# Down projection of a streaming encoder layer: block sums of its weight by accumulating DMAs one product ahead, first product a11 b11

## Chip, core and metric

One of the eight cores of one Trainium2 chip runs the whole kernel. The time is what the device takes for one execution, in microseconds (us). The kernel before was run three times: 1790.78 us in the median, 1787.89 to 1794.69 us. A further execution was profiled. TensorE (PE) multiplies, VectorE (DVE), ScalarE (ACT) and GpSimd (POOL) work on tiles, and SyncE (SP) issues most of the DMAs.

## What is computed

One inference layer over 1024 prompt tokens and 32 sample tokens, T = 1056 together, width 1024, in float32. The change lies in the last matmul of the feed-forward block (FFN):

```
h = h + a @ w_o
f = rmsnorm(h)
gc = causal_dwconv3(f @ w_g)
y = (gelu(gc) * (f @ w_u)) @ w_d
h = h + y
h = h + (p @ w_pe) * sigmoid(rmsnorm(h) @ w_pg)
```

w_d has 2816 rows and 1024 columns. Everything before and after this matmul computes the same in both kernels.

## The kernel before

The activations lie transposed: features on the 128 partitions, tokens along a row. A float32 operand is split into two parts, hi (ACT, `split_x`, line 255) and lo = x - hi (DVE, line 256), and a product of two operands is three matmuls, hi hi, hi lo and lo hi (`mm3`, lines 248 to 250).

The FFN loop makes the rows of the hidden layer, 22 tiles of 128 features (`ly`), two per block. The matmul with w_d is a Strassen-Winograd product of 2 by 2 blocks: even and odd row tiles of w_d against its even and odd column tiles, and even and odd feature tiles against the two halves of the tokens (HT = 528 each). It takes seven products instead of eight. Their right-hand operands (b11, b21, b22 and the sums t1, t2, t3, t4) are made by DVE at the end of each FFN block (lines 1307 to 1310) and stored by SP to the scratch tensor `d_q`. Their left-hand operands are blocks of w_d and sums of blocks.

The stage runs over `PRODUCTS`, in each over four units u (two column tiles of w_d, so two tiles `hT[2u]`, `hT[2u+1]` of h), in each over two halves of 264 tokens, and in each over 11 feature pairs k, three matmuls each. So a unit is 66 matmuls and a product 264. One half of a unit fills one PSUM tile `gt` (three of them); then it is added into h or into `rr[u]`, which holds the product a11 b11 and what is added to it later.

- **Rows** of the next product, 11 of 264 KB, are loaded by `stage` into tiles M (`mtile`, three) and T (`stg`, four) and split by `split_row`. DVE's part of a split is ordered behind the last addition of a unit (`behind`): rows 0 to 3 behind unit 1, 4 to 7 behind unit 2, 8 to 10 behind unit 3.
- **Weights** of a unit, 704 KB, come by `raw_w` into two `wraw` tiles or one `wr` tile. Products t1 and t3 start a sum tile `wsum[u]` by one DMA and add a second block with POOL (`add_w`, line 1397); t2 and b22 add one more block each. `product_w` does this at the beginning of the unit that uses it, then splits the sum into six hi and six lo tiles, enough for two units.
- **h** was stored to `d_h` before the FFN. `hT`, the tile T, `r2` (which holds `rr[2]` and `rr[3]`) and the pool of `wsum` lie in memory that the tiles of the FFN held (`lps.close()`), so nothing is put there before the last `d_q` store has landed. `rr[0]` and `rr[1]` lie elsewhere.

A scheduler orders each engine's instructions by a simulated time line. Each engine, and SP as issuer of DMAs, then works in its order.

Of the kernel before, what the change touches and what calls it, by code (L numbers as in the profile page):

```python
# [9 lines left out]
F32 = mybir.dt.float32  # L10
F32R = mybir.dt.float32r
I32 = mybir.dt.int32
AF = mybir.ActivationFunctionType
ALU = mybir.AluOpType
AX = mybir.AxisListType

SEQ, DEC, D, PAST, FF, PED = 1024, 32, 1024, 2048, 2816, 256
T = SEQ + DEC
# [5 lines left out]
NB = NF // 2  # L24
HT = T // 2
# [57 lines left out]
def layer_kernel(ctx: ExitStack, tc: tile.TileContext, I, O):  # L83
# [26 lines left out]
    def load(out, in_):  # L110
        nc.sync.dma_start(out=out, in_=in_)
# [22 lines left out]
    def copy(out, in_):  # L134
        return S.activation(out, in_, AF.Copy)  # L135

    def after(ins, other):

        tc.add_manual_dep(ins.ins, other.ins.name,
                          mybir.DependencyInfo(mybir.DependencyClass.NoSync, mybir.DependencyReason.DATA),  # L140
                          reason="order")
        return ins
# [109 lines left out]
    def split_x(hi, lo, src, scale=None):  # L252

        if scale is None:
            S.activation(hi, src, AF.Copy)
            return V.tensor_tensor(out=lo, in0=src, in1=hi.bitcast(F32), op=ALU.subtract)  # L256
        else:
            S.activation(hi, src, AF.Copy, scale=scale)
            return V.scalar_tensor_tensor(out=lo, in0=src, scalar=scale, in1=hi.bitcast(F32),  # L259
                                   op0=ALU.mult, op1=ALU.subtract)  # L260

    def fm(get, j, xs, c0, n):

# [1012 lines left out]
    for b in range(NF // 2):  # L1276
        wg = strassen_w(I["w_g"][0], b * 256)
        gg = [ytile(1060) for _ in range(2)]
        for j in range(2):
            ft = 2 * b + j  # L1280
            V.memset(gg[j][:, 0:2], 0.0)
            V.tensor_copy(gg[j][:, 1026:1028], convw[:, 66 + ft:110:NF])
        strassen(wg, ops, put_rows([g[:, 2:1060] for g in gg], 2))
        ys = []
        for j in range(2):
            ft, g = 2 * b + j, gg[j]
            V.tensor_copy(cout[:, 0:2, ft], g[:, 1024:1026])
            V.tensor_copy(cout[:, 2:4, ft], g[:, 1058:1060])
            y = ytile(1060)[:, 0:1058]
            V.tensor_scalar(out=y, in0=g[:, 0:1058], scalar1=convw[:, ft:ft + 1], scalar2=convb[:, ft:ft + 1],  # L1290
                            op0=ALU.mult, op1=ALU.add)
            V.scalar_tensor_tensor(out=y, in0=g[:, 1:1059], scalar=convw[:, NF + ft:NF + ft + 1], in1=y,
                                   op0=ALU.mult, op1=ALU.add)
            V.scalar_tensor_tensor(out=y, in0=g[:, 2:1060], scalar=convw[:, 2 * NF + ft:2 * NF + ft + 1], in1=y,
                                   op0=ALU.mult, op1=ALU.add)
            S.activation(y, y, AF.Gelu_apprx_tanh)
            ys.append(y)
        wu = strassen_w(I["w_u"][0], b * 256)
        ss = [ytile() for _ in range(2)]
        strassen(wu, ops, put_rows(ss, 0))  # L1300
        for j, a, e, o in ((1, 0, HT, 0), (1, HT, SEQ, 0), (1, SEQ, T, 2), (0, 0, SEQ, 0), (0, SEQ, T, 2)):
            (V if b == NB - 1 else G).tensor_tensor(out=ss[j][:, a:e], in0=ss[j][:, a:e], in1=ys[j][:, a + o:e + o],
                                                    op=ALU.mult)

        (b11_, b12_), (b21_, b22_), (t3_, t1_) = ((x[:, 0:HT], x[:, HT:T]) for x in (ss[0], ss[1], ys[0]))
        t4_ = ys[1][:, 0:HT]
        V.tensor_tensor(out=t3_, in0=b22_, in1=b12_, op=ALU.subtract)
        V.tensor_tensor(out=t1_, in0=b11_, in1=b12_, op=ALU.subtract)
        V.tensor_tensor(out=b12_, in0=t3_, in1=b11_, op=ALU.add)
        V.tensor_tensor(out=t4_, in0=b12_, in1=b21_, op=ALU.subtract)  # L1310
        for n, x in ((0, ss[0]), (2, ss[1]), (4, ys[0])):
            load(q_rows(n, 2, b), x[:, 0:T].rearrange("p (n c) -> p n c", n=2))
        load(q_rows(6, 1, b), t4_.unsqueeze(1))

    ps = mt()
# [5 lines left out]

    PRODUCTS = ("b21", "b11", "t1", "t2", "b22", "t3", "t4")
    wsum = [None] * 4
    wv = I["w_d"][0].rearrange("(b j p) c -> j p b c", j=2, p=128)
    f2 = [None] * KD
# [39 lines left out]
    def split_row(n, b, raw, behind=None):  # L1367
        if n % 2 and b < 6:
            t = dn.tile([128, 2, HT], F32R, name="oq", tag="Q", bufs=6)
        else:  # L1370
            t = ap_.tile([128, 2, HT], F32R, name="oq", tag="A", bufs=16)
        ins = split_x(t[:, 0, :], t[:, 1, :], raw, -1.0 if PRODUCTS[n] == "t2" else None)
        if behind is not None:
            after(ins, behind)
        xo[n, b] = t

    nraw = [1]
# [14 lines left out]
        load(t.rearrange("p (k c) -> p k c", c=128), src)  # L1392
        return [t[:, 0:512], t[:, 512:1024], t[:, 1024:1408]]

    def add_w(dst, src):
        for x, y in zip(dst, src):
            G.tensor_tensor(out=x, in0=x, in1=y, op=ALU.add)
        return dst

    def product_w(n, u):  # L1400
        nm = PRODUCTS[n]
        if nm == "b21":
            w = raw_w(0, 1, u)
        elif nm == "b11":
            w = raw_w(0, 0, u)
        elif nm == "t4":
            w = raw_w(1, 1, u)
        elif nm == "t1":
            t = sb.tile([128, NB * 128], F32, name="wsum", tag="B", bufs=4)
            w = wsum[u] = add_w(raw_w(1, 0, u, own=t), raw_w(1, 1, u, wide=u % 2))  # L1410
        elif nm == "t2":
            w = add_w(wsum[u], raw_w(0, 0, u))
        elif nm == "b22":
            w = add_w(wsum[u], raw_w(0, 1, u))
        else:
            t = sb.tile([128, NB * 128], F32, name="wsum", tag="B", bufs=4)
            w = add_w(raw_w(1, 0, u, own=t), raw_w(0, 0, u, wide=u % 2))
        parts = []
        for x in w:
            c = x.shape[1]  # L1420
            hi = wp.tile([128, 512], F32R, name="whi", tag="hi", bufs=6)
            lo = wp.tile([128, 512], F32R, name="wlo", tag="lo", bufs=6)
            split_x(hi[:, :c], lo[:, :c], x)
            parts.append((hi, lo))
        return [tuple(y[:, k % 4 * 128:k % 4 * 128 + 128] for y in parts[k // 4]) for k in range(NB)]

    def acc_into(dst, src, op=ALU.add):
        return V.tensor_tensor(out=dst, in0=dst, in1=src, op=op)  # L1428

    for b in range(NB - 1):  # L1430
        stage(0, b)
    xo["raw", 0, NB - 1] = ss[1][:, 0:HT]
    for b in range(NB):
        split_row(0, b, xo.pop(("raw", 0, b)))

# [7 lines left out]

    for n, nm in enumerate(PRODUCTS):
        if n == 6:
            sbs.close()
            lp, ybufs = pool("last"), 5
        first = n == 0
        for u in range(4):
            ws = product_w(n, u)  # L1450
            he, ho = hT[2 * u], hT[2 * u + 1]
            if n < 2:
                m = 2 * u + n
                load(hT[m], d_h[m * 128:(m + 1) * 128, :])
            done = None
            for c0 in (0, SC):
                ps = gt(SC)
                mm3(ps, ws, [(xo[n, k][:, 0, c0:c0 + SC], xo[n, k][:, 1, c0:c0 + SC]) for k in range(NB)])
                a, b_ = slice(c0, c0 + SC), slice(HT + c0, HT + c0 + SC)
                if nm == "b21":  # L1460
                    done = acc_into(he[:, a], ps)
                elif nm == "b11":
                    copy(rr[u][:, a], ps)
                    done = acc_into(he[:, a], ps)
                elif nm == "t1":
                    acc_into(he[:, b_], ps)
                    done = acc_into(ho[:, b_], ps, ALU.subtract)
                elif nm in ("t2", "t3"):
                    done = acc_into(rr[u][:, a], ps)
                elif nm == "b22":  # L1470
                    done = acc_into(he[:, b_], ps)
                else:
                    acc_into(ho[:, a], ps, ALU.subtract)
            if nm == "t2":
                acc_into(he[:, HT:T], rr[u])
            elif nm == "t3":
                acc_into(ho[:, HT:T], rr[u], ALU.subtract)
                acc_into(ho[:, 0:HT], rr[u], ALU.subtract)
            if n < 6:

                for b in range(4 * u, min(4 * u + 4, NB)):
                    stage(n + 1, b)
                for b in range(4 * u - 4, min(4 * u, NB)):
                    if b >= 0:
                        split_row(n + 1, b, xo.pop(("raw", n + 1, b)), done)
            else:
                for m in ((0, 2), (4, 6), (1, 3), (5, 7))[u] if u < 3 else ():
                    fin(m)
# [64 lines left out]
```

## Time and profile before

| | |
|---|---|
| median of three runs | 1790.78 us |
| profiled execution, its own time | 1788.01 us |
| its span, first to last instruction | 1786.2 us |
| outside the span | 1.8 us |
| PE busy | 1734.9 us, 97% of the span |
| DVE busy | 1142.0 us, 64% |
| ACT busy | 764.5 us, 43% |
| POOL busy | 397.2 us, 22% |
| mean granted clock of TensorE | 0.991 of full speed |

Busy shares are means over stages. A matmul's own time overlaps the next one's, so idle time of PE and the granted clock tell more than its busy share. Times in the rows below count from the start of the span.

### The profile page before, as it was taken

Reading aid. Unit: us, or ns where it says so; the run is one execution under the profiler, and the core shown is the slowest. Engines: PE = TensorE matmul, PEld = TensorE weight load, DVE = VectorE, ACT = ScalarE, POOL = GpSimd, SP = SyncE. Lnnn points to the kernel's source line nnn. Section 1 sums busy time; section 2 is a strip of 40 time slices with the busy share of each in tenths; the row PEclk is TensorE's granted clock in tenths of the full one; section 3 lists DMA queues with packets and bytes.
Section 4 is the critical chain, followed back from the end, with each engine's and each line's share of the span. In section 5 each row is a group of like instructions: output and inputs, shape, how many; then the busy total and the mean of one; then the engine's idle time right before and its main releaser. Section 6 shows DMA issues by size and latency. Waiting matters only on the chain. (4 is left out here: it accounts for less than half of the span.)

```text
span 1786.2 us, 32756 instructions
## 1 busy us (share of the span) xinstructions
PE 1734.9 (97%) x12890; PEld 1704.0 (95%) x12890; DVE 1142.0 (64%) x2428; ACT 764.5 (43%) x1726; POOL 397.2 (22%) x410
## 2 busy tenths in 40 slices
PE   7999999999999999999999999999999889989998
PEld 6998999999999999999999999999999888989998
DVE  7766766666664564565468876666666647757643
ACT  6536564656324434322346444343433433334332
POOL 5110001000121021000002434444334006331111
PEclk9999999999999999999999999999999989999999
DMA  8311222212222214544453332223332596662431
GB/s 287 101 54 41 72 72 76 82 66 78 85 65 68 80 52 168 177 144 148 153 168 109 103 102 90 90 91 109 111 117 79 184 324 198 186 193 76 135 121 49
DMA packets 191822, 210.17 MB, mean 118 GB/s; under 512 B 11229, under 2 KB 156981, under 8 KB 191669
## 3 DMA queue, kind: packets, MB, share of 16 engines
q1 hardware_dynamic: 174936, 177.52, 31.7%
q0 software_dynamic: 8896, 26.06, 4.2%
q10 hardware_dynamic: 7837, 4.51, 0.9%
q8 instruction: 101, 1.65, 0.4%
q14 instruction: 52, 0.43, 0.1%
HBM read 151.99 MB, written 56.06 MB: 116 GB/s over the span
## 5 line engine op out<-in xcount | busy, mean ns | idle before, releaser
L248 PE MATMUL gt<-apair,whi 128*128 128x352 f32 x672 | 220.0, 328 | 0.1
L249 PE MATMUL gt<-apair,whi 128*128 128x352 f32 x672 | 219.3, 327 | 0.0
L250 PE MATMUL gt<-apair,wlo 128*128 128x352 f32 x672 | 218.7, 326 | 0.0
L1183 DVE TENSOR_TENSOR wlo<-wraw,whi 128x512 fp32r<-128x512 f32 x154 | 142.0, 930 | 91.8 <-ACT whi L1182 91.7
L248 PE MATMUL gt<-oq,whi 128*128 128x264 f32 x616 | 177.4, 291 | 16.9 <-DVE hT L1428 11.2
L249 PE MATMUL gt<-oq,whi 128*128 128x264 f32 x616 | 179.1, 292 | 11.6 <-DVE oq L256 10.8
L250 PE MATMUL gt<-oq,wlo 128*128 128x264 f32 x616 | 177.6, 290 | 0.0
L1182 ACT ACTIVATE whi<-wraw 128x512 fp32r<-128x512 f32 x154 | 96.3, 632 | 158.7 <-PE st L1224 66.5
L1223 PE MATMUL gt<-opt,whi 128*128 128x264 f32 x528 | 149.7, 284 | 0.7 <-ACT whi L1182 0.4
L1224 PE MATMUL gt<-opt,whi 128*128 128x264 f32 x528 | 149.9, 284 | 0.0
L1225 PE MATMUL gt<-opt,wlo 128*128 128x264 f32 x528 | 149.7, 284 | 0.0
L248 PE MATMUL gt<-whi,apair 128*128 128x256 f32 x512 | 147.1, 289 | 0.6 <-ACT whi L221 0.6
L250 PE MATMUL gt<-whi,apair 128*128 128x256 f32 x512 | 146.9, 287 | 0.9 <-POOL apair L384 0.6
L249 PE MATMUL gt<-wlo,apair 128*128 128x256 f32 x512 | 146.9, 287 | 0.0
L248 PEld LDWEIGHTS gt<-oq,whi 128*128 128x128 f32 x616 | 118.8, 194 | 17.9 <-DVE hT L1428 11.9
L249 PEld LDWEIGHTS gt<-oq,whi 128*128 128x128 f32 x616 | 119.2, 194 | 13.9 <-DVE oq L256 12.8
L250 PEld LDWEIGHTS gt<-apair,wlo 128*128 128x128 f32 x672 | 126.6, 188 | 1.9 <-issue 0.2
L249 PEld LDWEIGHTS gt<-apair,whi 128*128 128x128 f32 x672 | 126.6, 188 | 1.4
L248 PEld LDWEIGHTS gt<-apair,whi 128*128 128x128 f32 x672 | 126.2, 188 | 1.7 <-DVE etile L782 0.3
L250 PEld LDWEIGHTS gt<-oq,wlo 128*128 128x128 f32 x616 | 119.3, 194 | 0.2 <-DVE wlo L256 0.2
L221 ACT ACTIVATE whi<-wraw 128x512 fp32r<-128x512 f32 x152 | 91.8, 629 | 63.0 <-PE gt L249 58.5
L222 DVE TENSOR_TENSOR wlo<-wraw,whi 128x512 fp32r<-128x512 f32 x152 | 103.7, 702 | 14.8 <-ACT whi L221 11.8
(455 smaller groups left out, 5209.6 us busy)
## 6 DMA issues: line engine op xcount, KB each, us to landing
d_q<-ly SPq DMA_DIRECT2D x33, 528.0 KB, 3.7
wraw<-in_w_in SPq DMA_DIRECT2D x28, 512.0 KB, 3.9
wraw<-in_w_g SPq DMA_DIRECT2D x22, 512.0 KB, 3.9
wraw<-in_w_u SPq DMA_DIRECT2D x22, 512.0 KB, 4.3
mtile<-d_q SPq DMA_DIRECT2D x36, 264.0 KB, 3.3
d_gt<-etile POOLq DMA_DIRECT2D x48, 176.0 KB, 2.1
ly<-d_gt SPq DMA_DIRECT2D x16, 528.0 KB, 3.6
wr<-in_w_d SPq DMA_DIRECT2D x12, 704.0 KB, 6.9
```

What stands on the lines that cost most here:

```text
L221: S.activation(hi, r, AF.Copy)
L222: V.tensor_tensor(out=lo, in0=r, in1=hi.bitcast(F32), op=ALU.subtract)
L248: PE.matmul(ps, wh, xh, start=first and i == 0, stop=False)
L249: PE.matmul(ps, wh, xl, start=False, stop=False)
L250: PE.matmul(ps, wl, xh, start=False, stop=last and i == n - 1)
L1182: S.activation(h3, src, AF.Copy)
L1183: V.tensor_tensor(out=l3, in0=src, in1=h3.bitcast(F32), op=ALU.subtract)
L1223: PE.matmul(ps, wh[:, ws], xh, start=start and k == 0, stop=False, skip_group_check=True)
L1224: PE.matmul(ps, wh[:, ws], xl, start=False, stop=False, skip_group_check=True)
L1225: PE.matmul(ps, wl[:, ws], xh, start=False, stop=k == n - 1, skip_group_check=True)
```

## The change

- The first product is b11 instead of b21. It is only copied into `rr[u]` by ACT; before, b11 came second, was copied and also added to h. Now b21 comes second, is added to h, and at the end of each unit `rr[u]` is added to h in one piece. So no `hT` is needed in the first product.
- The last row of the first product is taken from SBUF: `ss[0]` instead of `ss[1]`, and the products of the hidden layer are made for `ss[0]` first.
- POOL adds no weight blocks. `w_sums` loads the first block into `wsum[u]` by SP and adds the other by a DMA on POOL's queue that accumulates into the tile. It is called one product before the sum is used, behind the split of the same unit.
- `split_x` returns both instructions, so that a row of the second product is ordered on ACT behind ACT's copy of the first.

```diff
-        for j, a, e, o in ((1, 0, HT, 0), (1, HT, SEQ, 0), (1, SEQ, T, 2), (0, 0, SEQ, 0), (0, SEQ, T, 2)):
+        for j, a, e, o in ((0, 0, HT, 0), (0, HT, SEQ, 0), (0, SEQ, T, 2), (1, 0, SEQ, 0), (1, SEQ, T, 2)):
...
-    PRODUCTS = ("b21", "b11", "t1", "t2", "b22", "t3", "t4")
+    PRODUCTS = ("b11", "b21", "t1", "t2", "b22", "t3", "t4")
...
-            after(ins, behind)
+            after(ins[behind[0]], behind[1])
...
-    def add_w(dst, src):
-        for x, y in zip(dst, src):
-            G.tensor_tensor(out=x, in0=x, in1=y, op=ALU.add)
-        return dst
+    def w_sums(n, u):
+
+        def block(i, j):
+            return wv[j][:, :, u * 256 + i * 128:u * 256 + i * 128 + 128]
+
+        nm = PRODUCTS[n]
+        if nm in ("t1", "t3"):
+            wsum[u] = sb.tile([128, NB * 128], F32, name="wsum", tag="B", bufs=4)
+        elif nm not in ("t2", "b22"):
+            return
+        t = wsum[u].rearrange("p (k c) -> p k c", c=128)
+        if nm in ("t1", "t3"):
+            load(t, block(1, 0))
+        G.dma_start(out=t, in_={"t1": block(1, 1), "t2": block(0, 0), "b22": block(0, 1), "t3": block(0, 0)}[nm],
+                    accum_op=ALU.add)
...
-        elif nm == "t1":
-            t = sb.tile([128, NB * 128], F32, name="wsum", tag="B", bufs=4)
-            w = wsum[u] = add_w(raw_w(1, 0, u, own=t), raw_w(1, 1, u, wide=u % 2))
-        elif nm == "t2":
-            w = add_w(wsum[u], raw_w(0, 0, u))
-        elif nm == "b22":
-            w = add_w(wsum[u], raw_w(0, 1, u))
         else:
-            t = sb.tile([128, NB * 128], F32, name="wsum", tag="B", bufs=4)
-            w = add_w(raw_w(1, 0, u, own=t), raw_w(0, 0, u, wide=u % 2))
+            w = [wsum[u][:, 0:512], wsum[u][:, 512:1024], wsum[u][:, 1024:1408]]
...
-    xo["raw", 0, NB - 1] = ss[1][:, 0:HT]
+    xo["raw", 0, NB - 1] = ss[0][:, 0:HT]
...
             ws = product_w(n, u)
             he, ho = hT[2 * u], hT[2 * u + 1]
+            w_sums(n + 1, u) if n < 6 else None
             if n < 2:
                 m = 2 * u + n
                 load(hT[m], d_h[m * 128:(m + 1) * 128, :])
...
                 elif nm == "b11":
-                    copy(rr[u][:, a], ps)
-                    done = acc_into(he[:, a], ps)
+                    done = (0, copy(rr[u][:, a], ps))
...
-            if nm == "t2":
+            if nm == "b21":
+                done = (1, acc_into(he[:, 0:HT], rr[u]))
+            elif nm == "t2":
                 acc_into(he[:, HT:T], rr[u])
```

The scheduler's order changes with it. First SP's queue at the end of the FFN; `d_q<-ly` is the last store of the hidden layer, `wr` and `wraw` are weights, `mtile` and `stg` rows. Before:

```order
L111 DMA d_q<-ly 128x528
L111 DMA hT<-d_h 128x1056
L111 DMA stg<-d_q 128x528 x2
L111 DMA hT<-d_h 128x1056
L111 DMA stg<-d_q 128x528 x2
L111 DMA hT<-d_h 128x1056 x3
L111 DMA wr<-in_w_d 128x11x128
L111 DMA hT<-d_h 128x1056 x3
L111 DMA wsum<-in_w_d 128x11x128 x4
L111 DMA wraw<-in_w_d 128x8x128
```

And in the changed kernel, a part of the same place, from the fifth `hT` on:

```order
L111 DMA hT<-d_h 128x1056
L111 DMA wr<-in_w_d 128x11x128
L111 DMA wsum<-in_w_d 128x11x128
L111 DMA stg<-d_q 128x528
L111 DMA mtile<-d_q 128x528
L111 DMA stg<-d_q 128x528
L111 DMA hT<-d_h 128x1056
L111 DMA wraw<-in_w_d 128x8x128
L111 DMA mtile<-d_q 128x528
```

Rows and weights of the second product now lie between the `hT` and `wsum` loads instead of behind all of them; the last `mtile` here is that product's last row.

The second place is PE at the beginning of the second product in the changed kernel. The numbers tell the PSUM tiles apart: 17121 and 17156 are the halves of unit 0, 17218 is the first half of unit 1, and `oq_17092` is row 8.

```order
L250 MATMUL gt_17218<-oq_17002,wlo_17207 128x264
L248 MATMUL gt_17121<-oq_17092,whi_17113 128x264
L248 MATMUL gt_17156<-oq_17092,whi_17113 128x264
L248 MATMUL gt_17218<-oq_17092,whi_17210 128x264
L249 MATMUL gt_17121<-oq_17092,whi_17113 128x264
L250 MATMUL gt_17121<-oq_17092,wlo_17114 128x264
```

Ahead of them stand rows 0 to 7 of all three tiles, 72 matmuls; before, the second product's halves went one after the other, 33 matmuls each, from unit 1 on, with two in turn at its beginning.

The third place is POOL, the whole of the down stage, as a piece of the difference:

```order
 L114 DMA out_conv_sample<-mtile 44x128
-L1397 TENSOR_TENSOR wsum<-wsum,wraw 128x512 x2
-L1397 TENSOR_TENSOR wsum<-wsum,wraw 128x384
-L1397 TENSOR_TENSOR wsum<-wsum,wr 128x512 x2
-L1397 TENSOR_TENSOR wsum<-wsum,wr 128x384
+L1408 DMA wsum<-in_w_d 128x11x128 x16
 L979 TENSOR_TENSOR ly<-ly 128x1056 x5
```

Two of sixteen such groups of additions are shown; all 48 additions are gone, and sixteen DMAs stand in their place.

## Rows read from the trace of the kernel before

**Rows 1.** The page, its part 1: busy time of each engine in the whole span.

```profile
PE 1734.9 (97%) x12890; PEld 1704.0 (95%) x12890; DVE 1142.0 (64%) x2428; ACT 764.5 (43%) x1726; POOL 397.2 (22%) x410
```

**Rows 2.** Busy time by stretches, with granted clock, DMA share and GB/s last.

```profile
core 0: us, PE busy (x) PEld busy (x) DVE busy (x) ACT busy (x) POOL busy (x), PEclk, DMA share, GB/s
1400.00:1420.00 20.00, 20.00 (x167) 20.00 (x166) 16.67 (x32) 8.48 (x16) 1.09 (x2) 1.00 0.50 158
1426.50:1458.00 31.50, 22.86 (x165) 22.65 (x165) 8.82 (x17) 5.35 (x10) 0.00 (x0) 0.83 1.03 320
1458.00:1495.00 37.00, 36.36 (x280) 36.37 (x280) 22.65 (x32) 18.44 (x37) 15.77 (x12) 0.92 0.78 236
1563.00:1576.00 13.00, 8.89 (x58) 8.20 (x57) 8.05 (x11) 4.63 (x9) 4.39 (x3) 0.88 0.55 154
1603.00:1614.00 11.00, 7.62 (x46) 6.98 (x45) 7.85 (x11) 4.08 (x8) 3.14 (x2) 0.84 0.72 211
```

**Rows 3.** Time line of PE, its first two waits in the down stage (start, us, instruction).

```profile
1430.65 0.59 PE L248 MATMUL gt<-oq,whi 128*128 128x264 f32 x1 [10.20 <-DVE hT L1428]
...
1458.64 0.56 PE L248 MATMUL gt<-oq,whi 128*128 128x264 f32 x1 [5.13 <-issue]
```

**Rows 4.** Time lines of DVE, SP and ACT around those two waits.

```profile
1430.17 0.77 DVE L1428 TENSOR_TENSOR hT<-hT,gt 128x264 f32<-128x264 f32 x2 [9.46 <-DMA hT<-d_h]
...
1426.47 0.34 SPq L111 DMA_DIRECT2D hT<-d_h  x1
...
1426.43 0.64 ACT L255 ACTIVATE oq<-mtile 128x528 fp32r<-128x528 f32 x1 [7.82 <-DMA d_q<-ly]
...
1457.91 1.15 ACT L255 ACTIVATE whi<-wraw 128x512 fp32r<-128x512 f32 x2 [19.96 <-DMA wraw<-in_w_d]
```

**Rows 5.** Time line of PE, waits at the beginnings of products t1, t2, b22, t3.

```profile
1496.61 0.39 PE L249 MATMUL gt<-oq,whi 128*128 128x264 f32 x1 [0.80 <-DVE oq L256]
1498.31 0.39 PE L249 MATMUL gt<-oq,whi 128*128 128x264 f32 x1 [1.06 <-DVE oq L256]
1503.00 0.39 PE L249 MATMUL gt<-oq,whi 128*128 128x264 f32 x1 [2.48 <-DVE oq L256]
1536.53 0.39 PE L249 MATMUL gt<-oq,whi 128*128 128x264 f32 x1 [0.71 <-DVE oq L259]
1571.22 0.39 PE L249 MATMUL gt<-oq,whi 128*128 128x264 f32 x1 [3.40 <-DVE oq L256]
1572.92 0.59 PE L249 MATMUL gt<-oq,whi 128*128 128x264 f32 x1 [0.72 <-DVE oq L256]
1606.95 0.39 PE L248 MATMUL gt<-oq,whi 128*128 128x264 f32 x1 [0.99 <-DVE hT L1428]
1610.38 0.59 PE L249 MATMUL gt<-oq,whi 128*128 128x264 f32 x1 [2.20 <-DVE oq L256]
```

**Rows 6.** Time lines of DVE and POOL at the beginning of product t3.

```profile
1601.13 0.70 DVE L256 TENSOR_TENSOR oq<-stg,oq 128x528 fp32r<-128x528 f32 x1
1601.75 1.79 DVE L256 TENSOR_TENSOR oq<-mtile,oq 128x528 fp32r<-128x528 f32 x1
1603.47 1.80 DVE L256 TENSOR_TENSOR oq<-stg,oq 128x528 fp32r<-128x528 f32 x1
...
1601.40 4.74 POOL L1397 TENSOR_TENSOR wsum<-wsum,wr 128x512 f32<-128x512 f32 x3 [10.21 <-DMA wsum<-in_w_d]
```

**Rows 7.** DMA issues: out and in, engine, count, KB each, median us to landing.

```profile
mtile<-d_q SPq DMA_DIRECT2D x36, 264.0 KB, 3.3
...
wsum<-in_w_d SPq DMA_DIRECT2D x8, 704.0 KB, 7.6
...
hT<-d_h SPq DMA_DIRECT2D x8, 528.0 KB, 7.9
```

**Rows 8.** Line 114, DMAs issued by POOL: durations in ns, min/median/max.

```profile
L114 POOL DMA_DIRECT2D out_y_prompt<-mtile x14: 750/784/789, 1699.2 to 1775.0; - x14
...
L114 POOL DMA_DIRECT2D out_y_sample<-mtile x7: 529/529/539, 1703.2 to 1774.5; - x7
```

**Rows 9.** Waits of all engines, 1380 to 1700 us: in total, times, longest.

```profile
ACT oq L255 <- DMA mtile<-d_q: 64.4, 19, 9.3
```

More of the change, by code (lines that the diff above doesn't have):

```diff
@@ L254, in split_x @@
         if scale is None:
-            S.activation(hi, src, AF.Copy)
-            return V.tensor_tensor(out=lo, in0=src, in1=hi.bitcast(F32), op=ALU.subtract)
-        else:
-            S.activation(hi, src, AF.Copy, scale=scale)
-            return V.scalar_tensor_tensor(out=lo, in0=src, scalar=scale, in1=hi.bitcast(F32),
-                                   op0=ALU.mult, op1=ALU.subtract)
+            return (S.activation(hi, src, AF.Copy),
+                    V.tensor_tensor(out=lo, in0=src, in1=hi.bitcast(F32), op=ALU.subtract))
+        else:
+            return (S.activation(hi, src, AF.Copy, scale=scale),
+                    V.scalar_tensor_tensor(out=lo, in0=src, scalar=scale, in1=hi.bitcast(F32),
+                                           op0=ALU.mult, op1=ALU.subtract))
     def fm(get, j, xs, c0, n):
@@ L1393, in raw_w @@
         return [t[:, 0:512], t[:, 512:1024], t[:, 1024:1408]]
-    def add_w(dst, src):
-        for x, y in zip(dst, src):
-            G.tensor_tensor(out=x, in0=x, in1=y, op=ALU.add)
-        return dst
+    def w_sums(n, u):
[11 more added lines that the diff above has]
+                    accum_op=ALU.add)
     def product_w(n, u):
         nm = PRODUCTS[n]
[L1402 to L1407, printed above, removed]
-        elif nm == "t1":
-            t = sb.tile([128, NB * 128], F32, name="wsum", tag="B", bufs=4)
-            w = wsum[u] = add_w(raw_w(1, 0, u, own=t), raw_w(1, 1, u, wide=u % 2))
-        elif nm == "t2":
-            w = add_w(wsum[u], raw_w(0, 0, u))
-        elif nm == "b22":
-            w = add_w(wsum[u], raw_w(0, 1, u))
-        else:
-            t = sb.tile([128, NB * 128], F32, name="wsum", tag="B", bufs=4)
-            w = add_w(raw_w(1, 0, u, own=t), raw_w(0, 0, u, wide=u % 2))
+        if nm in ("b11", "b21", "t4"):
+            w = raw_w(*{"b11": (0, 0), "b21": (0, 1), "t4": (1, 1)}[nm], u)
+        else:
+            w = [wsum[u][:, 0:512], wsum[u][:, 512:1024], wsum[u][:, 1024:1408]]
         parts = []
@@ L1460, in layer_kernel @@
                 if nm == "b21":
-                    done = acc_into(he[:, a], ps)
+                    done = (1, acc_into(he[:, a], ps))
                 elif nm == "b11":
-                    copy(rr[u][:, a], ps)
-                    done = acc_into(he[:, a], ps)
+                    done = (0, copy(rr[u][:, a], ps))
                 elif nm == "t1":
                     acc_into(he[:, b_], ps)
-                    done = acc_into(ho[:, b_], ps, ALU.subtract)
+                    done = (1, acc_into(ho[:, b_], ps, ALU.subtract))
                 elif nm in ("t2", "t3"):
-                    done = acc_into(rr[u][:, a], ps)
+                    done = (1, acc_into(rr[u][:, a], ps))
                 elif nm == "b22":
-                    done = acc_into(he[:, b_], ps)
+                    done = (1, acc_into(he[:, b_], ps))
                 else:
                     acc_into(ho[:, a], ps, ALU.subtract)
-            if nm == "t2":
+            if nm == "b21":
+                done = (1, acc_into(he[:, 0:HT], rr[u]))
+            elif nm == "t2":
                 acc_into(he[:, HT:T], rr[u])
```

## The prediction

> **What bounds the kernel now.** I read the busy times first: PE is busy 97% of the span [rows 1], so only its idle time and a lowered clock can be won. PE's time line with gaps finds both in the down stage, and nearly nowhere else near the change. A matmul there takes 20.00 / 167 = 0.12 us at the full clock [rows 2].
>
> - The first wait is 10.20 us, up to 1430.65, and ends on an addition into h [rows 3]. DVE waited for the load of `hT`; SP issued that load at 1426.47, and ACT, which wanted a tile in the same memory, waited until 1426.43 for the last `d_q` store [rows 4]. So the memory of the FFN comes free at 1426.4, and `hT` one load later. PE had stopped at 1430.65 - 10.20 = 1420.45 with all three PSUM tiles full and none emptied, 99 of the first product's 264 matmuls.
> - The second wait is 5.13 us, up to 1458.64 [rows 3]. The profile calls it issue, but 0.7 us before its end ACT splits a weight tile for which it had waited 19.96 us [rows 4]. From 1426.5 to 1458 the DMA engines are full, share 1.03 at 320 GB/s [rows 2]. This stretch is bound by bytes, not by an engine.
> - Eight short waits lie at the beginnings of t1, t2, b22 and t3, 12.36 us in all, seven of them on DVE's split of a row [rows 5]. DVE takes 0.70 us for it, and 1.79 or 1.80 us beside a POOL addition [rows 6].
> - After waits PE runs slower: the granted clock is 0.83 and 0.92 in the first two stretches, 0.88 and 0.84 around b22 and t3 [rows 2]. Of the two levels, 1.2 and 2.4 GHz, that is 24% of 13 us and 32% of 11 us at 1.2 GHz, costing at most 1.6 and 1.8 us.
>
> **The change, part by part.** All times are against the profiled execution, 1788.0 us; the median of the three runs is 2.8 us above it.
>
> *First product.* Its 10.20 us go: the copies of units 0 and 1 need nothing of the freed memory, and unit 2's first copy is due at 1420.45 + 66 x 0.12 = 1428.4, after 1426.4. PE then ends b11 at 1420.45 + 165 x 0.12 = 1440.3. On ACT unit 3's copies stand behind splits of rows whose loads follow at most 2,376 KB after 1426.5; by the rate below they land by 1434.5, before that unit's first half ends at 1436.3.
>
> *Second product, what is late next.* The bytes do not go away. Before, SP moved eight `hT`, four rows, one `wr`, four `wsum` and a 512 KB `wraw` from 1426.47 to 1457.91 [rows 4], with the sizes of [rows 7] 9,312 KB in 31.4 us, 296 KB/us. In the new order 12,512 KB lie in SP's queue from the first `hT` to the last weights of b21: eight `hT`, twelve rows, four `wsum` and 2,304 KB of weights. That is 42.3 us. Beside it POOL's queue moves the other halves of t1's four sums, of which I count three and a half before those weights.
>
> What an accumulating DMA takes, no row shows. Not less than the plain load of the same 704 KB, 2.4 us at that rate; if it moves the bytes as a load, a second load and a store would, three times this. I take twice, a load and a read of the tile, being nearest to the plain load that [rows 7] has, and keep 1 and 3 as ends. With a factor m the sums add 3.5 x 2.4 x m = 8.3 m us. The last weights of b21 land at 1426.5 + 42.3 + 16.7 = 1485.5 (m = 2), PE starts on them 0.7 us later as in [rows 3, 4], and 66 matmuls and 1.5 us of lowered clock end b21 at 1495.6. For m = 1 it is 1487.2, for m = 3 1503.9. Before, t1 began 25 matmuls ahead of its first wait, 1496.61 - 0.80 - 3.0 = 1492.8 [rows 5]. So this part costs 2.8 us (from -5.6 to +11.1): the long first wait comes back as several waits in b21. PE's new order softens it, 72 matmuls of three tiles ahead of row 8.
>
> The DMA share of 1.03 [rows 2] leaves nothing for a second queue. The rule beside it, which speaks against the change, is in the Trainium skill ("DMA: Bandwidth & Descriptors", "Issuing engines are not separate DMA queues"): DMAs issued by different engines run on the same DMA engines and interleave. If POOL's queue had bandwidth of its own, b21 would end 16.7 us sooner and the forecast be 1764 us; by the rule it stays at the sum below. The Trainium skill ("Collectives: The Full Stack", "The bandwidth ceiling: the fold count and why AG ≠ RS ≠ AR") also says that a DMA that reduces reads two sources and so delivers at half the rate of a copy; no row here shows it, and by it m would be 2.
>
> *t1's beginning.* Its last row lies 16,032 KB into SP's queue, 54.2 us, with four sums 19.0 us more: 1499.7, and PE wants it 72 matmuls into t1, at 1504.2. So 0.80 + 1.06 + 2.48 = 4.3 us go [rows 5].
>
> *t2, b22, t3.* With no POOL addition running, each of the three or four late rows is split 1.1 us sooner [rows 6], as much as the gaps are long. That would win 0.7 us at t2, 4.1 + 1.6 at b22, 3.2 + 1.8 at t3, the clock included. Some rows also wait for their load [rows 9], so of the 10.7 us at b22 and t3 I take 8, with 4 and 10.7 as ends.
>
> *Costed at nothing.* The 48 POOL additions themselves: POOL is waited for next to never. Sixteen DMA issues: 0.53 us for 32 runs and 0.78 for 512 [rows 8] give about 1.3 us for 1,408 runs, on an idle POOL. DVE trades eight additions of 264 columns for four of 528. In the FFN, POOL's other order of products lies beside a PE that is busy 20.00 of 20 us [rows 2]; if that cover went, one 528-column product per block would be late. At its end the last chain of DVE is no longer, so 1426.4 stays.
>
> *Sum.* +2.8 - 4.3 - 0.7 - 8.0 = -10.2: 1777.8 for an execution like the profiled one, 1780.6 as a median. I say **1780 us**.
>
> **Rivals.**
>
> 1. *The accumulating DMAs become the bound (slower).* In the 31.7 us of a product (264 x 0.12) the DMA engines must carry eleven rows, 9.8 us, and four sums, 9.5 m us. They can up to m = 2.3. From there the excess falls on three products in which sums are fetched: at m = 3 38.3 us each, 3 x 6.6 = 20 us late, with b21's 11.1 and 4 won at b22 and t3: 1788.0 + 27 + 2.8 = 1818 us. For it: runs of only 512 B, and the stretch that is full already [rows 2]. Against: from 1563 on the DMA share is 0.55 to 0.72 with the same number of blocks loaded plainly. Chance 0.16.
> 2. *The waits only move (same).* b21 waits as computed, and rows at b22 and t3 are late by their loads, not by DVE: ACT waited 64.4 us for such loads [rows 9], 19 times. Then 2.8 - 4.3 - 0.7 = -2.2: 1789 us. Against: the 1.79 us beside POOL stands where the gap is. Chance 0.22.
> 3. *The change does not do what it says.* ACT's copies of unit 3 are stuck behind row splits whose loads land late, and PE still waits in the first product. Two spare PSUM tiles cover 8 us, so it would take landings 10 us later than computed; a wait of 5 us there then cuts those in b21, and 1785 us result. Chance 0.07.
>
> **How the numbers follow.** The forecast has 0.55. Its own range goes from m = 1 with all of 10.7 won, -5.6 - 4.3 - 0.7 - 10.7 = -21.3, 1770 us, to -2, 1789 us. The range for 8 in 10 goes lower by what the lowered clock may not take, 1766, and up to the first rival at m = 2.5: b21 ends at 1499.7, +6.9, three products 1.9 us late each, +5.7, less 0.7 and 4: 1799, so 1798. Left out are most of rival 1 and a little below. A measurement of this kernel tells about 0.5%, 9 us, from no change. Faster by more: five sixths of the forecast, 0.46. Within: the rest of it, rival 2 and most of 3, 0.37. Slower: rival 1 and a little, 0.17.
>
> **What would show it.** PE's time line should have no wait before 1440; then three to five waits of 2 to 7 us in b21, on rows 8 to 10 and weights whose loads landed late, with the DMA share near 1 up to 1485; t1 beginning between 1487 and 1500 without a wait; row splits on DVE at 0.70 us throughout; at most 3 us idle at b22 and t3 together. The accumulating DMA's time to landing against the 7.6 us of `wsum` [rows 7] gives m. I am wrong if PE still waits at 1420, if t1 begins after 1505, or if ACT waits for a sum in t2 or b22.

## The result and the profile after

The changed kernel takes 1778.17 us in the median of six runs (1775.60 to 1781.74), the kernel before 1790.11 us beside it: a ratio of 0.9933, with a 95% interval from 0.9913 to 0.9953. That is 0.67% or 12 us. Its profiled execution took 1778.33 us with a span of 1776.6, 9.6 us shorter than before. The busy times, against [rows 1]:

```profile
PE 1734.0 (98%) x12890; PEld 1702.7 (96%) x12890; DVE 1116.5 (63%) x2424; ACT 763.7 (43%) x1726; POOL 362.3 (20%) x378
```

PE does the same work. POOL's additions of weights, 66 us, are gone, and 31 us of issuing the sixteen DMAs stand in their place. DVE loses 25 us, 17 of them in the row splits counted below. Busy time by stretches, against [rows 2]; granted clock, DMA share and GB/s stand last:

```profile
1420.00:1440.00 20.00, 20.00 (x167) 20.00 (x166) 8.78 (x14) 8.77 (x18) 0.00 (x0) 1.00 0.91 300
1426.50:1458.00 31.50, 26.99 (x201) 25.83 (x199) 10.63 (x17) 10.38 (x22) 4.00 (x2) 0.95 1.09 298
1458.00:1495.00 37.00, 28.19 (x209) 27.45 (x210) 16.90 (x31) 11.69 (x22) 5.75 (x3) 0.91 1.23 265
1563.00:1576.00 13.00, 12.82 (x106) 12.61 (x105) 7.54 (x14) 5.59 (x11) 1.94 (x1) 1.00 0.89 166
1603.00:1614.00 11.00, 11.00 (x89) 11.00 (x89) 4.71 (x9) 4.94 (x9) 0.00 (x0) 0.96 0.28 85
```

The first product is clean: 20.00 of 20 us busy up to 1440, at full clock. In the next two stretches the DMA engines are fuller than before: a share of 1.09 goes with 298 GB/s, where 1.03 went with 320, and 1.23 with 265, where 0.78 went with 236. In the second of them PE does 209 matmuls where it did 280. At b22's beginning PE is busy 12.82 of 13 us, where it was busy 8.89. The last window held t3's beginning before (7.62 of 11 us); now that beginning lies a few us ahead of it, so its 11.00 of 11 us do not tell of t3's wait. PE's time line names the waits, against [rows 3, 5]:

```profile
1448.63 0.39 PE L248 MATMUL gt<-oq,whi 128*128 128x264 f32 x1 [2.87 <-ACT whi L255]
...
1463.20 1.03 PE L248 MATMUL gt<-oq,whi 128*128 128x264 f32 x3 [6.45 <-ACT oq L255]
...
1476.19 0.39 PE L248 MATMUL gt<-oq,whi 128*128 128x264 f32 x1 [1.28 <-ACT whi L255]
...
1482.22 0.39 PE L248 MATMUL gt<-oq,whi 128*128 128x264 f32 x1 [2.11 <-ACT whi L255]
...
1501.58 0.81 PE L248 MATMUL gt<-oq,whi 128*128 128x264 f32 x2 [2.08 <-ACT oq L255]
...
1533.81 0.39 PE L249 MATMUL gt<-oq,whi 128*128 128x264 f32 x1 [1.77 <-DVE oq L259]
...
1565.77 0.39 PE L249 MATMUL gt<-oq,whi 128*128 128x264 f32 x1 [0.18 <-DVE oq L256]
...
1600.76 0.59 PE L249 MATMUL gt<-oq,whi 128*128 128x264 f32 x1 [2.61 <-DVE oq L256]
```

The 10.20 us in the first product are gone. In their place b21 waits 13.1 us (the first four, and 0.22 us after the first and after the fourth, of which the expectations below left out one), t1 2.1, t2 1.8, b22 0.2 and t3 2.6 us. ACT's time line says what the waits up to t1 end on: loads that land late, for which ACT stands still and keeps what is queued behind.

```profile
1461.39 1.15 ACT L255 ACTIVATE whi<-wraw 128x512 fp32r<-128x512 f32 x2 [7.01 <-DMA wraw<-in_w_d]
...
1475.62 0.52 ACT L255 ACTIVATE whi<-wraw 128x384 fp32r<-128x384 f32 x1 [9.58 <-DMA wraw<-in_w_d]
...
1481.54 0.63 ACT L255 ACTIVATE whi<-wr 128x512 fp32r<-128x512 f32 x1 [5.40 <-DMA wr<-in_w_d]
...
1500.88 0.64 ACT L255 ACTIVATE oq<-mtile 128x528 fp32r<-128x528 f32 x1 [5.69 <-DMA mtile<-d_q]
```

At t3, where DVE had taken 1.79 us for a row beside POOL [rows 6], each row now takes 0.70:

```profile
1600.00 0.70 DVE L256 TENSOR_TENSOR oq<-mtile,oq 128x528 fp32r<-128x528 f32 x1
1600.62 0.70 DVE L256 TENSOR_TENSOR oq<-stg,oq 128x528 fp32r<-128x528 f32 x1
```

Between 1425 and 1640 the trace of before has 20 row splits of over 1.0 us, 19.9 us more than 0.70 each in all; that of after has two, both of rows for the last product.

**Where the 9.6 us come from** is read best from two marks that every version has: DVE's fourth addition of a PSUM tile into `rstd_b` in t2, and the fourth in t3. Before:

```profile
1548.63 0.42 DVE L1428 TENSOR_TENSOR rstd_b<-rstd_b,gt 128x264 f32<-128x264 f32 x1
...
1624.35 0.42 DVE L1428 TENSOR_TENSOR rstd_b<-rstd_b,gt 128x264 f32<-128x264 f32 x1
```

After:

```profile
1545.87 0.42 DVE L1427 TENSOR_TENSOR rstd_b<-rstd_b,gt 128x264 f32<-128x264 f32 x1
...
1614.79 0.42 DVE L1427 TENSOR_TENSOR rstd_b<-rstd_b,gt 128x264 f32<-128x264 f32 x1
```

By the mark in t2 only 2.8 us of the 10.2 are left; the other 6.8 us are won between the marks, from t2 through b22 into t3 (75.7 us before, 68.9 after).

### The profile page after: what moved, and what is told of

Its sections match the earlier page's. It is cut to its first block, busy times and chain, and to the rows that moved or that the text cites. A ratio compares the mean times of both kernels' runs of the same rounds, so it can differ in the third digit from the quotient of the medians.

```text
span 1776.6 us, 32689 instructions
## 1 busy us (share of the span) xinstructions
PE 1734.0 (98%) x12890; PEld 1702.7 (96%) x12890; DVE 1116.5 (63%) x2424; ACT 763.7 (43%) x1726; POOL 362.3 (20%) x378
## 5 line engine op out<-in xcount | busy, mean ns | idle before, releaser
L1183 DVE TENSOR_TENSOR wlo<-wraw,whi 128x512 fp32r<-128x512 f32 x154 | 136.1, 892 | 89.0 <-ACT whi L1182 87.1
L248 PE MATMUL gt<-oq,whi 128*128 128x264 f32 x616 | 175.3, 291 | 15.9 <-ACT oq L255 8.5
L249 PE MATMUL gt<-oq,whi 128*128 128x264 f32 x616 | 177.3, 290 | 4.7 <-DVE oq L256 2.8
L222 DVE TENSOR_TENSOR wlo<-wraw,whi 128x512 fp32r<-128x512 f32 x152 | 104.0, 704 | 14.6 <-ACT whi L221 11.5
## 6 DMA issues: line engine op xcount, KB each, us to landing
wsum<-in_w_d POOLq DMA_DIRECT2D x16, 704.0 KB, 13.1
```

Source lines behind the costliest of these rows:

```text
L222: V.tensor_tensor(out=lo, in0=r, in1=hi.bitcast(F32), op=ALU.subtract)
L248: PE.matmul(ps, wh, xh, start=first and i == 0, stop=False)
L249: PE.matmul(ps, wh, xl, start=False, stop=False)
L1183: V.tensor_tensor(out=l3, in0=src, in1=h3.bitcast(F32), op=ALU.subtract)
```

## Experiments

Theory A: the second product is bound by the time of the DMA engines, of which an accumulating DMA takes more than two plain loads' worth; from t2 on, what is won is POOL's slowing of DVE. Theory B: b21's waits come from the order in SP's queue, and the sums cost nothing. All kernels are compared with the kernel before by ratio, since beside the experiments that kernel took 1791.4 to 1792.7 us and not 1790.1. The marks are those of the one profiled execution, which can lie some us off the median (for t1's sums by POOL 8 us below it).

| kernel | us | ratio | mark in t2 | mark in t3 | between |
|---|---|---|---|---|---|
| before | 1790.11 | 1 | 1548.6 | 1624.4 | 75.7 |
| after | 1778.17 | 0.9933 | 1545.9 | 1614.8 | 68.9 |
| order alone | 1782.42 | 0.995 | 1545.1 | 1624.5 | 79.5 |
| sums alone | 1787.6 | 0.9975 | 1553.7 | 1621.7 | 68.0 |
| second block plain | 1765.13 | 0.9848 | 1537.4 | 1602.9 | 65.5 |
| no second block | 1757.73 | 0.9809 | 1528.0 | 1594.1 | 66.0 |
| additions by DVE | 1771.86 | 0.9895 | 1535.2 | 1608.7 | 73.5 |
| POOL additions without a load | 1759.73 | 0.9832 | 1529.8 | 1596.6 | 66.8 |
| t1's sums by POOL | 1771.35 | 0.988 | 1535.3 | 1600.6 | 65.3 |
| t1's sums by DVE | 1767.36 | 0.9863 | 1534.2 | 1602.8 | 68.6 |
| the same, h late | 1761.89 | 0.983 | 1526.6 | 1600.4 | 73.8 |
| after, h late | 1772.83 | 0.9901 | 1540.3 | 1612.3 | 72.0 |
| after, old order in the FFN | 1778.61 | 0.9927 | 1546.9 | 1615.0 | 68.1 |
| after, long runs added | 1777.01 | 0.9913 | 1543.3 | 1613.0 | 69.8 |

**The order alone.** `w_sums` is taken out, `add_w` and the old `product_w` are back.

```diff
-            w_sums(n + 1, u) if n < 6 else None
+            w = wsum[u] = add_w(raw_w(1, 0, u, own=t), raw_w(1, 1, u, wide=u % 2))
```

> The order of the products alone: b11 first and copied out, sums by POOL additions as before. Theory A (the second product is bound by the DMA engines' time, and an accumulating DMA takes about 2.3 times a plain load there: 9.4% of 16 engines against 4.2% in the queue table): no wait in the first product, the waits inside b21, 12.9 us after the change, fall under 5 us, because the sums' bytes leave that stretch, and t1 begins by 1482; the waits at t1, t2, b22 and t3 come back at 10 to 16 us, beside POOL additions. Time 1775 to 1784, so about as fast as the whole change. Theory B (the waits in b21 come from the order of rows and h tiles in SP's queue, the sums cost nothing there and win at b22 and t3): waits in b21 stay at 10 to 14 us, and the time is 6 us or more above the changed kernel's, 1784 to 1790.

1782.42 us, ratio 0.995 (0.9934 to 0.9965). The first product has no wait; b21 waits 3.4 us; from t1 to t3 there are 15.9 us of waits, with 21 row splits of over 1.0 us up to there. That is theory A's course. Its factor of 2.3, though, sets against each other the whole queue of POOL in the two kernels, which before held no sums at all; the factor is measured below. The profiled run, the slowest of the six at 1786.9 us, is ahead of before by 3.6 us at the mark in t2, and has given all of that back at the mark in t3:

```profile
1545.05 0.41 DVE L1428 TENSOR_TENSOR rstd_b<-rstd_b,gt 128x264 f32<-128x264 f32 x1
...
1624.52 0.42 DVE L1428 TENSOR_TENSOR rstd_b<-rstd_b,gt 128x264 f32<-128x264 f32 x1
```

**The sums alone.** The old order of products and of the FFN's products, with `w_sums` in place of `add_w`.

```diff
-    PRODUCTS = ("b11", "b21", "t1", "t2", "b22", "t3", "t4")
+    PRODUCTS = ("b21", "b11", "t1", "t2", "b22", "t3", "t4")
```

> The accumulating DMAs alone: product b21 first, with h tiles needed at once as before. Theory A: the wait of 10.2 us at 1420 stays, the second product (now b11) waits more than before, as the sums take engine time in the same stretch, and b22 and t3 win 4 to 7 us: 1787 to 1798, not faster than before. Theory B (the sums are free where they lie and win at t1, b22 and t3): 10 us less than before minus nothing, 1780 to 1785.

1787.6 us, ratio 0.9975 (0.9965 to 0.9984). In us this is inside A's range at its lower end; by the ratio it is 1785.6 against 1790.1, between the ranges of A and B, and A's "not faster than before" failed by a little. The time alone decides nothing here, but PE's time line shows both halves of A's argument:

```profile
1429.32 0.59 PE L248 MATMUL gt<-oq,whi 128*128 128x264 f32 x1 [10.55 <-DVE hT L1427]
...
1471.30 0.56 PE L248 MATMUL gt<-oq,whi 128*128 128x264 f32 x1 [19.43 <-issue]
```

The second wait, 5.13 us in [rows 3], is 19.43 us: four accumulating DMAs now share the full stretch with h. From the mark in t2 to that in t3, 68.0 us against 75.7 give 7.7 us back. So each half of the change is a gain alone (0.50 and 0.25%), together 0.67%, and the two meet in the second product.

**The second block loaded plainly, and not loaded.** The first drops `accum_op`, so the second block overwrites the first one; the second drops the whole DMA. Both leave the sums out.

```diff
-                    accum_op=ALU.add)
```

> The changed kernel with the second block of each sum loaded plainly by the same DMA on POOL's queue, in place of being added: same bytes read, same order, same queue; the output leaves out the first block of each sum. Theory A: the waits in b21 fall from 12.9 to about 4 us (three and a half sums times 3.3 us of engine time less), t1 begins by 1482, and the waits of 2.08, 1.77 and 2.61 us at t1, t2 and t3 go for the most part: 1764 to 1770. The DMA's time to landing falls from 13.1 to 7 to 9 us, its engine time from 5.8 to about 2.5 us. Theory B: same waits, 1776 to 1780.

> The changed kernel without the second block's DMA: the sums are left out altogether. Theory A: not over 4 us faster than with the plain load, 1761 to 1768, since the DMA engines are then no longer full. Theory B: as the changed kernel, 1776 to 1780. If both fall together by under 3 us, the waits in b21 and at t1 are of the rows and h tiles alone.

1765.13 us (ratio 0.983 to 0.9865) and 1757.73 (0.9791 to 0.9826). Bytes, order and queues of the first are those of the changed kernel: the adding costs 13 us by the medians, 15 by the ratios, and theory B falls. The queue of these DMAs between 1420 and 1640 us (packets, MB, share of 16 engines) after, and with plain loads:

```profile
q0 software_dynamic: 22784, 11.54, 42.0%
```

```profile
q0 software_dynamic: 3072, 11.54, 18.9%
```

For 16 DMAs that is 0.42 x 220 / 16 = 5.78 us of the engines' time each, against 0.189 x 220 / 16 = 2.60: m is 2.2. The same 1,408 runs of 512 bytes were 192 packets a DMA in the plain load and 1,424 in the accumulating one. Two expectations failed. The waits in b21 fell to 8.0 us, not 4. And without the DMA 7.4 us more went, not under 4: with plain loads the DMA engines were still full from 1460 to 1500 us,

```profile
1460.00:1500.00 40.00, 36.13 (x271) 35.92 (x272) 21.65 (x38) 14.39 (x26) 4.31 (x4) 0.91 1.05 314
```

and without them not, and PE did not wait there:

```profile
1460.00:1500.00 40.00, 40.00 (x331) 40.00 (x330) 26.25 (x50) 16.83 (x31) 0.00 (x0) 1.00 0.66 198
```

**POOL or DVE for the additions.** Two kernels ask what cost the time from t2 on. In the first, the kernel with the order alone, DVE makes the additions:

```diff
-            G.tensor_tensor(out=x, in0=x, in1=y, op=ALU.add)
+            V.tensor_tensor(out=x, in0=x, in1=y, op=ALU.add)
```

> b11 first as in the changed kernel, every second block loaded plainly, and the additions made by DVE in place of POOL (48 more DVE instructions, about 0.7 us each for 512 columns, 33 us of DVE in all). Theory A (DMA time in b21, DVE slowed by POOL at the later boundaries): the waits in b21 stay at about 3 us as with POOL's additions, row splits take 0.70 us, and the waits at t1 to t3, 15 us there, fall to 6 to 10: 1770 to 1778, faster than the changed kernel. Rival: DVE's queue is in order, so row splits and evacuations stand behind additions that wait for their blocks: 1782 to 1792.

The second is the changed kernel without the second block's DMA, where POOL adds each block to itself at the old place in the program, so the sums are left out:

```diff
+            for x in w:
+                G.tensor_tensor(out=x, in0=x, in1=x, op=ALU.add)
```

> The changed kernel without the second block's DMA, with three POOL additions per unit in t1, t2, b22 and t3 that add a block to itself (no transfer behind them): the sums are left out, the additions stand at the old place. Theory A (POOL's additions slow DVE's row splits from 0.70 to 1.8 us, and this is what the boundaries t1 to t3 waited for before): row splits beside them take 1.7 to 1.9 us, waits at t1 to t3 of 8 to 14 us against 1.8 in the kernel without additions, 1766 to 1772. Rival (before, the rows were late by their loads, the slower split only stood beside that): waits under 4 us, 1757 to 1762.

By DVE 1771.86 us (0.988 to 0.991), 0.55% less than by POOL, with every row split up to t3's at 0.70 us: the slowing is real. But 12.2 us of waits stay from t1 to t3, more than expected, and between the marks it needs 73.5 us, where accumulating DMAs need 68.9. DVE's time line ahead of t3 shows one reason: an addition waits 1.45 us until its block has landed, and an evacuation, for which PE waits 1.59 us, and four rows stand behind it.

```profile
1584.32 0.69 DVE L1397 TENSOR_TENSOR wsum<-wsum,wr 128x512 f32<-128x512 f32 x1 [1.45 <-issue]
1584.92 0.42 DVE L1428 TENSOR_TENSOR hT<-hT,gt 128x264 f32<-128x264 f32 x1
1585.27 0.70 DVE L256 TENSOR_TENSOR oq<-mtile,oq 128x528 fp32r<-128x528 f32 x1
```

POOL's additions without a load went the rival's way: 1759.73 us (0.9816 to 0.9848), 66.8 us between the marks against 66.0 without additions. Thirteen row splits from b21 to t3 were slow, as here,

```profile
1572.73 1.55 DVE L256 TENSOR_TENSOR oq<-stg,oq 128x528 fp32r<-128x528 f32 x1
1574.20 1.54 DVE L256 TENSOR_TENSOR oq<-mtile,oq 128x528 fp32r<-128x528 f32 x1
```

and PE's only waits from t1 to t3 were 0.54, 0.98 and 1.24 us. So these slow splits cost next to nothing. But they took 1.1 to 1.55 us, not 1.8, and at t3 none fell on the last rows: with no second block to wait for, POOL's last addition ended at 1576.4, and PE's wait at t3 at 1583.9. This kernel also loads 11.5 MB less. It does not show what a slow split costs that falls on the last rows ahead of a product's beginning, because an addition is late; that is read from the trace of the kernel before. A split frees the buffer into which SP loads a later row. The split of 1601.75 in [rows 6] ends at 1603.54, and SP's time line has a row's load right behind it:

```profile
1603.62 0.32 SPq L111 DMA_DIRECT2D mtile<-d_q  x1
```

ACT's time line has that row 2.7 us later:

```profile
1606.34 0.64 ACT L255 ACTIVATE oq<-mtile 128x528 fp32r<-128x528 f32 x1 [1.84 <-DMA mtile<-d_q]
```

PE's wait of 2.20 us, up to 1610.38 [rows 5], is for another row, which ACT had split at 1603.86. DVE's half of it stands behind the split of weights, which ACT came to only after the late row:

```profile
1608.07 1.29 DVE L256 TENSOR_TENSOR wlo<-wsum,whi 128x512 fp32r<-128x512 f32 x2 [1.18 <-ACT whi L255]
...
1609.63 0.70 DVE L256 TENSOR_TENSOR oq<-mtile,oq 128x528 fp32r<-128x528 f32 x1
```

**Where in the stretch the sums hurt.** t1's four sums by plain loads and POOL additions a product later, the other twelve accumulating:

```diff
-        if nm in ("t1", "t3"):
+        if nm == "t3":
...
+            for x, y in zip(w, raw_w(1, 1, u, wide=u % 2)):
+                G.tensor_tensor(out=x, in0=x, in1=y, op=ALU.add)
```

> The changed kernel, but t1's four sums, which fall into the full stretch, by a plain load and POOL additions a product later as before; t2, b22 and t3 keep the accumulating DMAs. Theory A: the waits in b21 fall from 12.9 to 3 to 5 us, those at t1 and t2 rise from 4.2 to 5 to 8, b22 and t3 keep 2.8: 1769 to 1775, faster than both. Rival (the engine time of t2's accumulating DMAs, now beside t1's plain loads, only moves the wait one product on): 1776 to 1780.

1771.35 us (0.9862 to 0.9899; runs from 1763.15, the profiled one, to 1772.65). b21 waits 2.7 us, t1 7.5, then PE waits for nothing over 0.15 us until 0.56 at t4's beginning: theory A's course, and better at b22 and t3, where 2.8 us were expected to stay. The other four runs took 5 to 9.5 us longer, so waits of theirs are not in this trace. One row split at t1 took 4.52 us, beside three additions and an issue of POOL, and PE waited for it:

```profile
1483.87 4.52 DVE L256 TENSOR_TENSOR oq<-mtile,oq 128x528 fp32r<-128x528 f32 x1
```

```profile
1488.45 0.59 PE L249 MATMUL gt<-oq,whi 128*128 128x264 f32 x1 [3.14 <-DVE oq L256]
```

Then with t1's additions by DVE:

```diff
-                G.tensor_tensor(out=x, in0=x, in1=y, op=ALU.add)
+                V.tensor_tensor(out=x, in0=x, in1=y, op=ALU.add)
```

> As the kernel with t1's sums by POOL and the others by accumulating DMAs, but DVE makes t1's twelve additions. Theory A (POOL's additions slow DVE's row splits at t1; there the kernel waited 7.5 us): splits at 0.70 us in t1, waits at t1 of 2 to 4 us, b21 still 2 to 3, the rest under 2: 1763 to 1769, the fastest so far. Rival (the additions are late by their loads and DVE stands behind them): 1771 to 1776.

1767.36 us (0.9847 to 0.988), an interval that overlaps the one with POOL. With the same loads, t1's waits fall from 7.5 to 0.7 us, so at a product's beginning POOL's slowing does cost. But t2 and t3 wait more than expected, and at the mark in t2 only 1.1 us of it are left:

```profile
1520.49 0.59 PE L249 MATMUL gt<-oq,whi 128*128 128x264 f32 x1 [4.94 <-DVE oq L259]
...
1588.62 0.39 PE L249 MATMUL gt<-oq,whi 128*128 128x264 f32 x1 [2.55 <-DVE oq L256]
```

**Less h ahead of b21.** b21 and t1 write the even h tiles, and an accumulating DMA adds h to them after b22; once in the changed kernel, once in the last one.

```diff
-            if n < 2:
+            if n == 1:
...
+            if nm == "b22":
+                G.dma_start(out=he, in_=d_h[u * 256:u * 256 + 128, :], accum_op=ALU.add)
```

> The changed kernel without the loads of the four even h tiles ahead of b21 (2.1 MB): b21 and t1 write these tiles, and an accumulating DMA adds h after b22. Theory A (the bytes of the stretch set its waits): 7 us less of the DMA engines' time before t1, so waits in b21 of 4 to 8 us in place of 12.9, t1 begins 5 to 8 us sooner, and t3 and t4, where the DMA share is 0.3 to 0.5, take the additions without a wait: 1770 to 1775. Rival (waits are of rows and weights in SP's order, h is not among them): 1776 to 1780; if fin waits for h at t4's beginning: above 1780. The additions of h have rows of 4.2 KB: if the price lies in the 512-byte runs, they land like a plain load of 528 KB, 8 us; if it lies in the adding, in 13 us or more.

> The same, and the even h tiles by accumulating DMAs after b22 in place of loads ahead of b21. Theory A: with the sums gone from b21 the 2.1 MB less leave 0 to 2 us of its 2 to 3 us of waits, and the additions of h, beside t3's sums, cost 0 to 3 at b22 and t3: 1762 to 1770, the same as without within 3 us. Rival (bytes of h still set b21): 3 us or more faster than without.

1772.83 us (0.9884 to 0.9918), the time expected, but not in the way expected: in the profiled run, the second slowest of five at 1776.0 us, b21 waits 16.0 us, not 4 to 8, and the gain shows at t1 and t2. The additions of h, in rows of 4.2 KB, landed after 16.8 us in the median, which the expectation had put down to the adding, not to short runs; the long runs in the last experiment below landed after 8.8, so the landing settles nothing. The second is the fastest kernel of the study, 1761.89 us (0.9813 to 0.9848). It beats the one without late h by 5.5 us, more than the 3 from which the rival was to hold, but again not in b21 and t1 (4.8 us of waits against 3.5): the 4.94 us at t2 go, and t3 waits 5.48 us for its rows, beside the additions of h. Why less h helps t2 rather than b21 was not tried.

**Two terms by themselves.** The old order of the FFN's five products:

```diff
-        for j, a, e, o in ((0, 0, HT, 0), (0, HT, SEQ, 0), (0, SEQ, T, 2), (1, 0, SEQ, 0), (1, SEQ, T, 2)):
+        for j, a, e, o in ((1, 0, HT, 0), (1, HT, SEQ, 0), (1, SEQ, T, 2), (0, 0, SEQ, 0), (0, SEQ, T, 2)):
```

> The changed kernel with the five products of an FFN block in the old order (second half of rows first). The prediction costs this order at nothing, as PE is busy 20 of 20 us beside it: 1776 to 1780. Rival (b11's last row comes straight from this product and would be late): a wait in the first product near 1420, 1780 or more.

1778.61 us, ratio 0.9927 (0.9912 to 0.9943): this order is worth nothing, as costed. Its waits lie elsewhere, though: b21 waits 20.5 us, not 13.1, t1 and t2 not at all, and yet the mark in t2 is only 1.0 us later. So two kernels of one time divide their waits differently between b21, t1 and t2. And the accumulating DMA with long runs, which adds other data to each sum:

```diff
+        G.dma_start(out=wsum[u], in_=I["w_g"][0][u * 128:u * 128 + 128, 0:NB * 128], accum_op=ALU.add)
```

> The changed kernel, but each accumulating DMA adds 128 rows of 5.6 KB of another weight in place of 1,408 runs of 512 bytes: the same bytes added in long runs; the sums are of the wrong block. If the price of an accumulating DMA is that of its short packets: 170 to 190 packets a DMA in place of 1,424, engine time 2.5 to 3.3 us in place of 5.8, POOL's issue near 0.6 us, and 1763 to 1769 as with plain loads. If it is the adding itself (a second operand read and written): engine time 5 us or more and 1775 to 1780.

```profile
q0 software_dynamic: 2304, 11.54, 28.1%
```

144 packets a DMA, and 0.281 x 220 / 16 = 3.86 us of engine time, between the two guesses: of the 3.2 us above a plain load 1.9 go with the short packets, and 1.3 stay. A plain load of the long runs was not tried, so that these 1.3 are the adding's is not shown. And the time is 1777.01 us (0.9898 to 0.9928), within the uncertainty that of the changed kernel; b21 still waits 12.3 us, 3.88 of them on a weight load that ACT awaited for 14.60 us. So a third less engine time wins next to nothing: the engines' time, on which theory A rests, does not set the kernel's time by itself, and why an adding DMA costs 13 us more than a plain one stays open.

## Why the prediction was right, and where not

1780 us were forecast, in a range from 1766 to 1798; it is 1778.2, faster by more than 0.5%, the case that was given 0.46. For the profiled execution -10.2 us were worked out, and -9.6 measured. By its own steps:

- **First product, its 10.20 us gone.** Right. PE's 20.00 us of 20 up to 1440 are what was worked out, and ACT's copies were not stuck, so the third rival is out.
- **b21, +2.8.** Right in kind, 4.7 us too pessimistic. The waits came in b21, on late weights and a late row, four of 1.3 to 6.5 us. t1 began 72 matmuls ahead of the wait that started at 1501.58 - 2.08: at 1490.9, not 1495.6, against 1492.8 before. What failed is the stretch's limit: the share was not held at 1.03 but went to 1.23, and b21's last weights were split at 1481.5, not after 1485.5. Of the three and a half sums counted ahead of them only two had landed by then. The factor of 2 is near the 2.2 measured, but the long runs, at 1.5, took the same time, so its fit is in part luck.
- **m and the first rival.** The rival needed m above 2.3. At 2.2 it is near, and its count left something out: in b22 SP also loads t3's four first blocks, 2,816 KB beside the rows and sums. The DMA share of b22, over its 264 matmuls, was 0.67 before and is 1.04 after (1.07 in t1, 1.02 in t2):

```profile
1563.90:1602.30 38.40, 34.29 (x267) 33.60 (x265) 21.82 (x29) 11.94 (x22) 13.73 (x10) 0.96 0.67 189
```

```profile
1561.60:1594.20 32.60, 32.42 (x266) 32.21 (x265) 17.55 (x32) 12.16 (x22) 5.78 (x3) 1.00 1.04 201
```

The sentence of the Trainium skill ("Collectives: The Full Stack", "The bandwidth ceiling: the fold count and why AG ≠ RS ≠ AR") that a reducing DMA runs at half the rate of a copy gives 2 and lies close to the 2.2 measured; but 1.9 of the 3.2 us of difference went with the short packets, so the runs do not bear out the second read as the reason. That POOL's queue has no bandwidth of its own, as the Trainium skill says ("DMA: Bandwidth & Descriptors", "Issuing engines are not separate DMA queues"), is borne out: with POOL's DMAs left out the DMA share from 1460 to 1500 us is 0.66, with plain ones 1.05, and the kernel is 7.4 us faster.
- **t1, -4.3, and t2, -0.7.** These two terms failed. Both beginnings still wait, 2.1 and 1.8 us, now for rows whose loads land late. At t1 the late row was computed to land at 1499.7 and came to ACT at 1500.88; PE, ahead of plan after b21, wanted it at 1499.5 and not at 1504.2. The median landing of `mtile` between 1420 and 1640 us went from 3.2 us to 4.8:

```profile
mtile<-d_q SPq DMA_DIRECT2D x33, 264.0 KB, 4.8
```

- Together with b21 the sum to the mark in t2 is -2.8, against -2.2 worked out: two errors of opposite sign, which hang together. What PE did not lose in b21 it lost at t1 and t2, as it came sooner to rows that came no sooner; the kernel with the old order in the FFN, whose waits are all in b21, comes to the mark within 1.0 us.
- **b22 and t3, -8.0.** -6.8 measured. The size was near; the reason, that each late row is split 1.1 us sooner, was too narrow. Splits at 0.70 us alone, in the kernel with DVE's additions, bring the 79.5 us between the marks to 73.5, and without additions of its own the changed kernel needs 68.9. That the rest comes of additions that stand late in an engine's order is read from traces, and no run shows it by itself. ACT's waits for such rows hardly changed against [rows 9]:

```profile
ACT oq L255 <- DMA mtile<-d_q: 59.2, 20, 8.4
```

- The second rival's late loads are there, then, but at b22 and t3 they cost PE 0.2 and 2.6 us.
- **Costed at nothing.** The FFN's order: shown. POOL's issue was put at 1.3 us each and took 1.93:

```profile
L1408 POOL DMA_DIRECT2D wsum<-in_w_d x16: 1910/1926/2056, 1444.9 to 1595.6; - x16
```

POOL has nothing else to do there, and PE's waits end on rows and weights, none on a sum.

## What to carry to other kernels

A wait that is moved off one product by doing the loads' work later met the loads' bytes in the next one here: sum what every queue must carry up to the next deadline before counting the gain. Put accumulating DMAs where the DMA engines have room, and leave those that fall into a full stretch as plain loads with an addition on an engine with time: t1's four sums made so, and four loads of h moved behind, give 1761.9 us, 30 us less than before instead of 12. And an addition that waits for its block delays what is behind it by its lateness too: 1.45 us of waiting beside 0.69 of work, in the kernel with DVE's additions.

## What the runs showed of the hardware

An accumulating DMA of 1,408 runs of 512 bytes went out as 1,424 packets, a plain load of the same runs on the same queue as 192; engine time 5.8 and 2.6 us, landing 13.1 and 8.1 us, POOL's issue 1.93 and 1.08 us. With rows of 5.6 KB the accumulating one had 144 packets, 3.9 us, 8.8 us and 0.86 us. The DMA share went to 1.23 in a stretch where it delivered 265 GB/s, less than the 320 at 1.03 [rows 2]: a share says how long packets were under way, not what they bring.

DVE's split of a row took 0.70 us by itself and also beside POOL's issue of a DMA, up to 1.81 beside POOL's addition of two tiles, up to 1.55 beside the addition of a tile to itself, and once 4.52 beside three additions and an issue.
